# A decoder layer with split weights: weight units of 1024 columns, wider VectorE operations, an order from estimated clocks

## The chip, the cores and the metric

One core of one Trainium2 chip runs the whole layer in one launch. The metric is the device time of that core in microseconds; smaller is better. Four compute engines matter here: TensorE (matmuls and transposes), VectorE, ScalarE and GpSimd; SP's queue and ScalarE's queue issue the DMAs.

## The reference

One layer over 256 tokens and a model width of 2048, all in float32. What is computed, cut to its skeleton:

```python
h = layer_norm(alpha * x + 0.5 * swiglu(x, w_ffn1_gu, w_ffn1_down), ...)      # width 5632
rq, rk, rv, rg, aq, ak, av, gate_r, gate_a = split(h @ w_in)
rq, rk, aq, ak = rotary(...)                                                  # by positions
ret = (silu(rg) * head_group_norm(retention_chunkwise(rq, rk, rv))) @ w_ret_out   # 8 heads
att = sliding_window_attention_sinks(aq, ak, av, sinks) @ w_att_out               # 16 heads
h = layer_norm(alpha * h + (sigmoid(gate_r) * ret + sigmoid(gate_a) * att) @ w_mix_out, ...)
h = layer_norm(alpha * h + 0.5 * swiglu(h, w_ffn2_gu, w_ffn2_down), ...)
h = layer_norm(alpha * h + sigmoid(h @ w_ple_gate) * (p @ w_ple_proj), ...)
```

## The kernel before

**Split numbers.** Every weight and every activation is split into a high part (cast to the matmul's fp32r by ScalarE, line 93) and a low part (VectorE subtracts the high part from the original, line 94). A product of 128 rows, 128 tokens and 512 columns is three matmuls: low by high, high by high, high by low (`Sum.add`, lines 289 to 291). The first of the three needs the low part of the activations and the high part of the weights, the third needs the low part of the weights. All matmuls add in PSUM, one bank of 512 columns for each tile of 128 tokens (t = 0, 1) and block of columns.

**Chunks and sevens.** A weight chunk (`Chunk`) is 1024 values a partition, 4 KB: two rows of 128 by 512 columns. It is loaded by one DMA on SP's queue (line 107), cast and subtracted. A `Single` is one chunk and serves 12 matmuls. A `Seven` is two chunks that are used by a scheme of seven products in place of eight (21 matmuls in place of 24): it needs four sums of weights (lines 165 to 168) that are split too, and forms of the activations (`seven_forms`, lines 360 to 363). Its seven sums lie in the bank pairs of the block and in four banks more, named s; `seven_common` (lines 371 to 374) folds those. In the order of its steps p1, q2, q3, q5, p7, p6, q4, the sums p1, q5, p7 and p6 are the banks named s.

**Stages.** (1) The first feed-forward part, f1: block 0 with plain chunks, while x arrives in four pieces (`first_chunk`, `load_x_chunk`); ten blocks of 512 gate and 512 up columns with three or four sevens in eight (`gu_units`); after each block Silu, a product, and a transposition of the result two side steps later (`turned`: transposes on line 717, ScalarE's copy f1a on line 719). Then two down blocks d0 and d1 with sevens (`down_units`), the last pieces of which are held for the norm. (2) The norm, then the mixers: values (rv), eight groups of queries and keys (rqk) that are rotated (`rotate`: ScalarE copies, VectorE shuffles, GpSimd multiplies), the other values, the retention's gates (rg) with the retention's jobs as side steps, attention's queries and keys (aqk), the gates gt with attention's jobs as side steps, the output projections, and the mix (mo). (3) Norm 1, the second feed-forward part f2, norm 2, the gated embedding (pg), the last norm and the output.

**What sets the order.** The order is written by hand: each engine takes its instructions in the order in which the program issues them, and an engine that waits holds all that stands behind it. `fill` loads and converts chunks ahead of their use. It goes on as long as places of 4 KB are free under a limit that each stage sets (`slots_for_weights`), up to 45 us of TensorE work converted and 90 us loaded. `done` gives places back. `run_side` issues one side job after each chunk; the tables for the rotation (`rotary_tables`, lines 631 to 658, tiles rotr and rota) run there from block 0 of f1 on.

**The norms** (`Norm`). The last three pairs of rows of d1 (six chunks), or the last six chunks of the mix, are held: first all products of token tile 0, then those of tile 1. Behind the first half stand the combination with the residual, the statistics, the moments (`ln_stats`, a chain of nine small operations) and the scaling (`ln_normal`, lines 471 and 472) of tile 0. Its transposes (`ln_turn`, line 479, tile lnps) stand at fixed places among the products of tile 1, and those of tile 1 among the first six chunks of the next stage (`Norm.first`). Each transposed group is split into the activations of the next stage (ht). Between a norm and the mixers, and between norm 1 and f2, stands the projection of p (`put_by`, 24 matmuls).

Places: 46 of 4 KB in SBUF, and PSUM's eight banks as eight single tiles.

Of the kernel before, what the change touches and what calls it, by code (L numbers as in the profile page):

```python
# [8 lines left out]
F32 = mybir.dt.float32  # L9
# [17 lines left out]
KF = FF // P  # L27


HELD_MIX, HELD_END = 6, 8  # L30
FRONT = 6
FRONT_PAIRS = 3
HELD_PAIRS = 3
SLOTS = 46


SEVEN = (0, 1, 2, 3)


# [9 lines left out]

@with_exitstack  # L50
def layer(ctx: ExitStack, tc: tile.TileContext, io):
    nc = tc.nc
    sync, act, dve, pool, pe = nc.sync, nc.scalar, nc.vector, nc.gpsimd, nc.tensor
# [4 lines left out]
    small = ctx.enter_context(tc.tile_pool(name="small", bufs=3))  # L58
    dram = ctx.enter_context(tc.tile_pool(name="dram", bufs=1, space=bass.MemoryType.DRAM))
    psum = ctx.enter_context(tc.tile_pool(name="psum", bufs=8, space=PSUM))  # L60

    def bank(name):
        return psum.tile([P, 512], F32, tag="ps", name=name)

    def banks(name):
        return [bank(name + str(j)) for j in range(2)]
# [4 lines left out]
    def half(name):  # L71
        return slot([P, 2, 256], F32, name)

    plan = []

    def chunk_of(key):


        name, at = key[0], key[1:]
        if name.endswith("_gu"):
            j, gu, c = at
            w = io[name][2 * j : 2 * j + 2, gu, c // 2, :, c % 2 * 2 : c % 2 * 2 + 2, :]
            return w.rearrange("g p k n -> p g (k n)")
        if name[-1] == "2":
            j, c = at
            w = io[name[:-1]][j : j + 2, c // 2, :, c % 2 * 2 : c % 2 * 2 + 2, :]
            return w.rearrange("g p k n -> p g (k n)")
        return io[name][at]  # L90

    def split(dst_hi, dst_lo, src, lo_engine=None):
        act.copy(dst_hi, src)  # L93
        (lo_engine or dve).tensor_tensor(dst_lo, src, dst_hi, ALU.subtract)  # L94

    class Chunk:


        def __init__(self, key, pieces=1, queue=None):
            src = chunk_of(key)  # L100
            self.key, self.paired = key, key[0].endswith("_gu") or key[0][-1] == "2"
            self.name = "_".join(map(str, key))
            self.raw = slot(list(src.shape), F32, "r" + self.name)
            n = src.shape[2] // pieces
            self.parts = [slice(j * n, j * n + n) for j in range(pieces)]
            for at in self.parts:
                (queue or sync).dma_start(self.raw[:, :, at], src[:, :, at])

        def make_hi(self):
            self.hi, self.lo = (slot(list(self.raw.shape), F32R, w + self.name) for w in "hl")  # L110

        def make_part(self, at):
            split(self.hi[:, :, at], self.lo[:, :, at], self.raw[:, :, at])

        def make(self):
            self.make_hi()
            split(self.hi, self.lo, self.raw)

        def of(self, v, kk):

            if self.paired:
                return v.rearrange("p g (k n) -> p g k n", k=2)[:, :, kk, :]
            return v[:, kk, :]

        def columns(self, kk):
            return self.of(self.hi, kk), self.of(self.lo, kk)

    class Single:


        loads, makes, keeps, time = 1, 2, 2, 12

        def __init__(self, key):
            self.key = key

        def load(self, **how):
            self.chunk = Chunk(self.key, **how)

        def make(self):
            self.chunk.make()  # L140

    class Seven:

        loads, makes, keeps, time = 2, 6, 7, 21

        def __init__(self, key, other):
            self.key, self.other = key, other  # L150

        def load(self):
            self.a, self.b = Chunk(self.key), Chunk(self.other)

        def make(self):
            a, b = self.a, self.b
            nm = a.name
            b11, b21, b12, b22 = a.of(a.raw, 0), a.of(a.raw, 1), b.of(b.raw, 0), b.of(b.raw, 1)
            u, v = (slot([P, 2, 512], F32, w + nm) for w in "uv")

            def shaped(x):
                return x.rearrange("p (g n) -> p g n", g=2) if a.paired else x

            t1, t3, t2, t4 = (shaped(x) for x in (u[:, 0], u[:, 1], v[:, 0], v[:, 1]))
            dve.tensor_tensor(t1, b11, b12, ALU.add)
            dve.tensor_tensor(t3, b12, b22, ALU.add)  # L166
            dve.tensor_tensor(t2, b11, t3, ALU.add)
            dve.tensor_tensor(t4, t2, b21, ALU.add)  # L168

            def parted(name, x):  # L170
                hi, lo = (slot([P, 2, 512], F32R, w + name + nm) for w in "hl")
                split(hi, lo, x)
                return [(hi[:, e], lo[:, e]) for e in range(2)]

            a.make()
            self.b11, self.b21 = a.columns(0), a.columns(1)
            both = slot([P, 2, 512], F32R, "b" + nm)
            self.b22 = both[:, 0], both[:, 1]
            split(shaped(both[:, 0]), shaped(both[:, 1]), b22)
# [27 lines left out]
    def take(key):  # L207
        if not ready:
            fill()
# [1206 lines left out]
```

## Time and profile before

| what | value |
|---|---|
| runs, us | 2327.76, 2331.27, 2330.24 |
| median, us | 2330.24 |
| profiled execution: span from the first to the last instruction, us | 2330.8 |
| its granted TensorE clock, mean | 0.992 |
| instructions | 28659 |
| DMA moved | 465.70 MB, mean 200 GB/s |

For the profiled execution the span is the only time that is on record; it lies among the three runs. The page of the profile gives busy times by engine, the stretch of the span cut in 40 slices, the chain of work that ended last and the costliest groups. In a group's row stand line, engine, operation, the tile written and those read (buffer numbers left out), shape, count, then busy time, mean duration of one and the idle time before them. A row of waits has the engine and line that waited, whom it waited for, the total, the number of times and the longest. A row of stages has the stretch, its length, for each engine its busy time and number of instructions, the granted clock, the DMA share and GB/s. A row of the timeline has the start, the time, and the instruction; a bracket names idle time before it.

### The profile page before, as it was taken

How to read it: one execution, taken by the hardware profiler on the slowest of the kernel's cores; microseconds unless marked ns; L12 is line 12 of the kernel's file. 1: busy time of each engine (PE TensorE's matmuls, PEld its weight loads, DVE VectorE, ACT ScalarE, POOL GpSimd, SP SyncE). 2: the span in 40 equal slices, each digit the busy share in tenths (PEclk: the TensorE clock that was granted, in tenths of full speed). 3: DMA queues.
4: the chain of work that ended last, by engine and by line, in shares of the span. 5: the costliest groups of instructions: out<-in, count | busy, mean ns of one | idle time of the engine just before them, and what ended most of it. 6: DMA issues, size and time to landing. Idle time of an engine off the chain costs nothing.

```text
span 2330.8 us, 28659 instructions
## 1 busy us (share of the span) xinstructions
PE 2286.1 (98%) x10490; PEld 1890.7 (81%) x10490; DVE 1884.6 (81%) x2372; ACT 1167.0 (50%) x1412; POOL 97.0 (4%) x53
## 2 busy tenths in 40 slices
PE   9999999999998999999999999999999999999997
PEld 7788888887887888888778888778888888878776
DVE  7999999988978774677655555779999999899866
ACT  5555555655544342434554543355555555555432
POOL 0000000000000530133000000000000000000000
PEclk9999999999999999999999999999999999999999
DMA  9465665664686565546555666576566666465851
GB/s 321 156 215 181 207 205 184 198 217 159 220 296 234 179 226 163 171 144 201 158 158 181 190 207 228 183 245 214 183 190 208 185 206 227 166 210 204 329 190 55
DMA packets 193725, 465.70 MB, mean 200 GB/s; under 512 B 14768, under 2 KB 16048, under 8 KB 193584
## 3 DMA queue, kind: packets, MB, share of 16 engines
q1 hardware_dynamic: 191456, 460.91, 59.7%
q10 hardware_dynamic: 2128, 2.97, 0.4%
q8 instruction: 82, 1.34, 0.2%
q14 instruction: 59, 0.48, 0.1%
HBM read 455.43 MB, written 8.39 MB: 199 GB/s over the span
## 4 chain that ended last, share of the span: by engine, by line
PE 93%; DVE 5%; DMA 1%; issue 1%; ACT 0%; SPq 0%; DVEq 0%; ACTq 0%
PE f2g L291 3%; PE f2g L289 3%; PE f2g L290 3%; PE f1g L289 3%; PE gt L289 3%; PE f1g L290 3%; PE f1g L291 3%; PE rqk L240 3%; PE gt L290 3%; PE gt L291 3%; PE f2u L289 2%; PE f2u L290 2%; PE f2u L291 2%; PE f1u L291 2%; PE f1u L289 2%; PE f1u L290 2%
## 5 line engine op out<-in xcount | busy, mean ns | idle before, releaser
L94 DVE TENSOR_TENSOR lf_gu<-rf_gu,hf_gu 128x1024 fp32r<-128x1024 f32 (+1 forms) x283 | 335.1, 1215 | 11.5 <-ACT hf_gu L93 10.9
L93 ACT CAST hf_gu<-rf_gu 128x1024 fp32r<-128x1024 f32 (+1 forms) x283 | 282.9, 1046 | 17.1 <-DMA rf_gu<-in_f_gu 13.3
L94 DVE TENSOR_TENSOR lw_in_f<-rw_in_f,hw_in_f 128x1024 fp32r<-128x1024 f32 x148 | 208.2, 1439 | 61.7 <-ACT hw_in_f L93 58.5
L94 DVE TENSOR_TENSOR lf_down<-rf_down,hf_down 128x1024 fp32r<-128x1024 f32 x148 | 174.5, 1219 | 14.0 <-ACT hf_down L93 12.0
L93 ACT CAST hf_down<-rf_down 128x1024 fp32r<-128x1024 f32 x148 | 149.4, 1051 | 49.7 <-DMA rf_down<-in_f_down 9.9
L93 ACT CAST huf_gu<-uf_gu 128x1024 fp32r<-128x1024 f32 x70 | 73.8, 1054 | 160.1 <-DVE uf_gu L166 153.5
L93 ACT CAST hw_in_f<-rw_in_f 128x1024 fp32r<-128x1024 f32 x148 | 146.0, 1053 | 0.2
L289 PE MATMUL gt<-hw_in_f,ht 128*128 128x512 f32 x256 | 102.5, 400 | 0.0
L289 PE MATMUL f1g<-hf_gu,xt 128*128 128x512 f32 x247 | 97.0, 393 | 5.5 <-ACT hf_gu L93 5.5
L290 PE MATMUL gt<-hw_in_f,ht 128*128 128x512 f32 x256 | 99.9, 390 | 0.0
L291 PE MATMUL gt<-lw_in_f,ht 128*128 128x512 f32 x256 | 99.9, 390 | 0.0
L290 PE MATMUL f1g<-hf_gu,xt 128*128 128x512 f32 x247 | 96.8, 392 | 0.0
L291 PE MATMUL f1g<-lf_gu,xt 128*128 128x512 f32 x247 | 96.6, 391 | 0.0
L289 PE MATMUL f2g<-hf_gu,ht 128*128 128x512 f32 x247 | 96.4, 390 | 0.0
L291 PE MATMUL f2g<-lf_gu,ht 128*128 128x512 f32 x247 | 96.2, 389 | 0.0
L290 PE MATMUL f2g<-hf_gu,ht 128*128 128x512 f32 x247 | 96.1, 389 | 0.0
L93 ACT CAST hvf_gu<-vf_gu 128x1024 fp32r<-128x1024 f32 x70 | 73.9, 1055 | 29.2 <-DVE vf_gu L168 29.2
L94 DVE TENSOR_TENSOR luf_gu<-uf_gu,huf_gu 128x1024 fp32r<-128x1024 f32 x70 | 85.3, 1219 | 0.0
L94 DVE TENSOR_TENSOR lvf_gu<-vf_gu,hvf_gu 128x1024 fp32r<-128x1024 f32 x70 | 85.3, 1219 | 0.0
L289 PE MATMUL f2u<-hf_gu,ht 128*128 128x512 f32 x212 | 84.0, 396 | 0.0
L289 PE MATMUL f1u<-hf_gu,xt 128*128 128x512 f32 x212 | 83.4, 393 | 0.0
L290 PE MATMUL f2u<-hf_gu,ht 128*128 128x512 f32 x212 | 83.0, 392 | 0.0
(1053 smaller groups left out, 6257.3 us busy)
## 6 DMA issues: line engine op xcount, KB each, us to landing
rf_gu<-in_f_gu SPq DMA_DIRECT2D x351, 512.0 KB, 5.0
rf_down<-in_f_down SPq DMA_DIRECT2D x176, 512.0 KB, 4.6
rw_in_f<-in_w_in_f SPq DMA_DIRECT2D x148, 512.0 KB, 4.2
rw_rv<-in_w_rv SPq DMA_DIRECT2D x32, 512.0 KB, 5.1
rw_ret<-in_w_ret SPq DMA_DIRECT2D x32, 512.0 KB, 4.5
rw_mix<-in_w_mix SPq DMA_DIRECT2D x32, 512.0 KB, 4.5
rw_pg<-in_w_pg SPq DMA_DIRECT2D x32, 512.0 KB, 4.4
rw_att<-in_w_att SPq DMA_DIRECT2D x16, 512.0 KB, 4.3
```

Source lines behind the costliest of these rows:

```text
L93: act.copy(dst_hi, src)
L94: (lo_engine or dve).tensor_tensor(dst_lo, src, dst_hi, ALU.subtract)
L240: pe.matmul(ps[f], hi[:, kk, f * P : (f + 1) * P], rhs(k), start=k == 0, stop=k == n_k - 1,)
L289: pe.matmul(o, al, bh, start=first, stop=False)
L290: pe.matmul(o, ah, bh, start=False, stop=False)
L291: pe.matmul(o, ah, bl, start=False, stop=self.left == 0)
```

## The change

- **Units.** SBUF has 23 places of 8 KB in place of 46 of 4 KB. A unit is 2048 values a partition: two rows of 128 by 1024 columns (both column blocks at once), loaded by two DMAs, or by four shorter-run ones for a seven of the gate and up weights; one cast of 2048, one subtraction of 2048, 24 matmuls. A seven's weights are made in four steps with wider operations. PSUM is four tiles of two banks.
- **Order.** Two estimated clocks, one for TensorE and one for VectorE, are advanced by the sizes of what is issued. Steps of the making of weights are issued while VectorE's clock is behind TensorE's (`pump`), and `after` does so up to the point at which a result of TensorE is expected, ahead of VectorE's work on it. At most three units are loaded ahead.
- **Norms.** What happens behind which held step is a list of events (c combine, m moments, s scale, t transpose, with token tile and group); groups are eight tiles of 128 wide, in norm 1 at first four. Three units are held, four of the next stage stand in front.
- **Moved.** The rotary tables go from f1's first blocks behind norm 0, into the remaining four units of the first value block. The rotation's products go from GpSimd to VectorE, the retention's product with its gate goes to VectorE and ScalarE. The load of p goes from SP's queue at the norm to ScalarE's queue at the start.
- **Start and end.** The first unit comes in four pieces on ScalarE's queue, interleaved with x's first four; other units wait in SP's queue behind x's chunks. At the end five units are held; tile 0 finishes 1024 columns behind them, tile 1 twice 512.

The number of matmuls and transposes stays, and so do the sevens (`SEVEN`, `SEVEN_DOWN`, `SEVEN_BOTH`).

The core of the diff:

```diff
-SLOTS = 46
+SLOTS = 23
+FRONT = 4
+HELD = 3
+HELD_END = 5
+MATMUL = 0.227
+GROUPS = (((0, 8), (8, 8)), ((0, 8), (8, 8)), ((0, 4), (4, 4), (8, 8)))
...
+EVENTS = (
+    {
+        "a6": "c0 m0 s00", "b6": "t00 c1 m1 s10", "c4": "s01", "c6": "t10", "d1": "s11", "d4": "t01", "d7": "t11",
+    },
...
+    {
+        "a6": "c0 m0 s00 s01", "b4": "t00", "b6": "t01 c1 m1 s10 s11", "c4": "s02", "c6": "t10", "c7": "t11",
+        "d1": "s12", "d4": "t02", "d7": "t12",
+    },
+)
...
-    psum = ctx.enter_context(tc.tile_pool(name="psum", bufs=8, space=PSUM))
+    psum = ctx.enter_context(tc.tile_pool(name="psum", bufs=4, space=PSUM))
...
+    def banks(name):
+        return psum.tile([P, 2, 512], F32, tag="ps", name=name)
...
+    class Unit:
+        loads, makes, keeps, steps = 1, 2, 2, 1
...
+        def make(self):
+            self.make_hi()
+            split(self.hi, self.lo, self.raw)
+            spend(2048)
+            yield
...
+    class Seven(Unit):
+        loads, makes, keeps, steps = 1, 5, 4, 4
...
+            act.copy(hb, raw[:, 1:])
+            dve.tensor_tensor(u[:, 0:2], raw[:, 1:3], raw[:, 0:1].broadcast_to([P, 2, 512]), ALU.add)
+            act.copy(hu[:, 0:2], u[:, 0:2])
+            spend(1024)
+            yield
+            dve.tensor_tensor(u[:, 2], raw[:, 2], u[:, 0], ALU.add)
+            dve.tensor_tensor(u[:, 3], u[:, 2], raw[:, 3], ALU.add)
+            act.copy(hu[:, 2:], u[:, 2:])
+            spend(512, 512)
+            yield
...
+            dve.tensor_tensor(lb, raw[:, 1:], hb, ALU.subtract)
+            spend(1536)
+            yield
+            dve.tensor_tensor(lu, u, hu, ALU.subtract)
+            spend(2048)
...
+    clock = {"pe": 0.0, "dve": 0.0}
+    room = {"slots": 0, "used": 0, "far": 3}
+    def spend(*sizes):
+        for n in sizes:
+            clock["dve"] += (n + 150) / 960
...
+    def pump(t):
+        load()
+        while clock["dve"] < t and step():
+            pass
+    def fill():
+        pump(clock["pe"])
+    def after(t=None):
+        t = clock["pe"] if t is None else t
+        pump(t)
+        clock["dve"] = max(clock["dve"], t)
+    def take(*key):
+        load()
+        while not ready:
+            assert step(), (key, room)
+        u = ready.pop(0)
+        clock["pe"] = max(clock["pe"], u.made)
+        return u
...
+            if aux is None:
+                pair = [banks(f"{name}{b}s{j}") for j in range(2)]
+                aux = p1, p6, p7, q5 = [Sum(pair[j // 2][:, j % 2], len(sevens)) for j in range(4)]
...
-            later(2, lambda j=j, v=v: turned(j, v))
+            later(1, lambda j=j, u=u: turned(j, u))
...
-                    if u == 2:
-                        load_constants()
-                        lazy.append(rotary_tables())
+                    if u == 2:
+                        load_constants()
...
+        def held(self, name, b, ps, lhs):
+            us = [take(name, b, p) for p in ps]
+            for j in range(2 * len(ps)):
+                at = j % len(ps)
+                some_products(us[at], ps[at], lhs, self.sums, (0,), (j // len(ps),))
+                fill()
+                run_side()
+                self.at("a", j + 1)
...
-        pool.tensor_tensor(q, q, c, ALU.mult)
-        pool.tensor_tensor(qs, qs, s, ALU.mult)
-        pool.tensor_tensor(dst, q, qs, ALU.add)
+        dve.tensor_tensor(q, q, c, ALU.mult)
+        dve.tensor_tensor(qs, qs, s, ALU.mult)
+        dve.tensor_tensor(dst, q, qs, ALU.add)
...
+        ps, sums = norm.front("w_rv", 0, rhs, plain(PAIRS))
+        lazy.append(rotary_tables())
+        plain_block("w_rv", 0, rhs, start=FRONT, sums=sums)
...
+                        dve.scalar_tensor_tensor(
+                            o[:, e, t], ps[:, e, t * DV : t * DV + DV], mv[:, j, 0:1], g, ALU.subtract, ALU.mult
+                        )
+                        act.mul(o[:, e, t], o[:, e, t], rs[:, j : j + 1])
```

1305 lines of the change are left out of this document (618 added, 687 removed).

## The prediction

> **What bounds the kernel now.** First the page's busy shares, then two matmuls of TensorE's timeline that stand 20 matmuls apart, then TensorE's waits.
>
> ```profile
> PE 2286.1 (98%) x10490; PEld 1890.7 (81%) x10490; DVE 1884.6 (81%) x2372; ACT 1167.0 (50%) x1412; POOL 97.0 (4%) x53
> ```
> ```profile
> 12.85 0.39 PE L289 MATMUL f1g<-hf_gu,xt 128*128 128x512 f32 x1
> ...
> 17.39 0.39 PE L291 MATMUL f1u<-lf_gu,xt 128*128 128x512 f32 x1
> ```
> ```profile
> PE lnps L479 <- DVE f2y L472: 6.6, 5, 3.8
> PE lnps L479 <- DVE f1y L472: 6.1, 4, 2.6
> ...
> PE f11s L289 <- ACT f1a L719: 5.3, 1, 5.3
> PE lnps L479 <- DVE mixy L472: 3.9, 4, 2.7
> ```
>
> A busy 0.39 hides pipelining: (17.39 - 12.85) / 20 = **0.227 us a matmul** of 512 columns. TensorE is nearly full, and its named waits are few: the three norms (transposes waiting for VectorE's scaled rows) and one in the first block with sevens. Now the stages.
>
> ```profile
> 5.00:50.00 45.00, 44.48 (x188) 36.31 (x189) 36.65 (x54) 24.98 (x29) 0.00 (x0) 1.00 0.96 333
> 50.00:75.00 25.00, 19.68 (x85) 15.95 (x84) 23.89 (x37) 13.56 (x18) 0.00 (x0) 0.93 0.40 138
> 100.00:500.00 400.00, 400.00 (x1807) 332.21 (x1806) 375.60 (x435) 227.27 (x258) 0.00 (x0) 1.00 0.62 199
> 555.00:600.00 45.00, 43.40 (x189) 34.97 (x188) 42.15 (x48) 24.87 (x27) 0.00 (x0) 1.00 0.68 232
> 700.00:740.00 40.00, 33.92 (x145) 26.73 (x144) 37.33 (x67) 17.08 (x25) 0.00 (x0) 0.87 0.47 169
> ...
> 1490.00:1525.00 35.00, 31.10 (x144) 24.50 (x143) 31.03 (x59) 17.00 (x28) 0.00 (x0) 0.95 0.52 178
> ...
> 2195.00:2240.00 45.00, 38.24 (x160) 30.05 (x159) 37.20 (x66) 12.22 (x17) 0.00 (x0) 0.89 0.68 244
> ```
>
> The columns: length, busy TensorE, weight loads, VectorE, ScalarE, GpSimd, granted clock, DMA share, GB/s. What a stage loses is its idle TensorE time plus (1 - clock) x length: 5.3 + 1.75 = **7.1** in 50 to 75, 6.1 + 5.2 = **11.3** in norm 0, 3.9 + 1.75 = **5.7** in norm 1, 6.8 + 5.0 = **11.7** in norm 2. That is 36 us, and nearly all that can be won in the middle: from 100 to 500 TensorE idles for nothing although VectorE is 94% busy. The diff keeps every matmul and transpose, so the rest of the span stands.
>
> **The change, part by part.** *Wider operations.* Rows of 512 and of 1024 give the slope.
>
> ```profile
> L94 DVE TENSOR_TENSOR lf_gu<-rf_gu,hf_gu 128x1024 fp32r<-128x1024 f32 x281 | 333.7, 1219 | 9.5 <-ACT hf_gu L93 9.0
> L93 ACT CAST hf_gu<-rf_gu 128x1024 fp32r<-128x1024 f32 x281 | 281.6, 1049 | 15.3 <-DMA rf_gu<-in_f_gu 11.5 <-PE mo L291 1.7 <-PE mo L290 1.4
> ...
> L165 DVE TENSOR_TENSOR uf_gu<-rf_gu,rf_gu 128x512 f32<-128x512 f32 x70 | 47.9, 685 | 0.0
> ...
> L93 ACT CAST bf_gu<-rf_gu 128x512 fp32r<-128x512 f32 x70 | 43.3, 619 | 0.0
> ```
>
> VectorE: 0.151 + 1.043 per 1000 elements, so 2048 take 2.29 and 1536 1.75; ScalarE: 1.91 and 1.48. A plain unit falls from 2 x 1.219 = 2.44 to 2.29, a seven from 7.1 (four of 0.69, four subtractions) to 1.22 + 1.38 + 1.75 + 2.29 = 6.64. Blocks of four sevens and blocks of three alternate: 85.1 us of VectorE a pair of blocks before, with the fold; 79.6 after. The 94% becomes 88%. **I cost this at nothing**: TensorE hid the greater load already. If a margin were lost, it would cost what the down stage loses (555 to 600: 1.6 idle), whose runs of three sevens I leave at 0 (-3 to +3): 6.64 against 21 x 0.227 = 4.77 of TensorE still falls behind there, with about one seven of lead, as now. DMAs carry the same bytes in shorter runs for the sevens; at a DMA share of 0.62 I take 0, and no more than a few us if the share rose to 0.96.
>
> *First block.* The first unit comes in four pieces and needs two for its first product, and each later unit is cast whole.
>
> ```profile
> 4.85 0.62 ACT L93 CAST hf_gu<-rf_gu 128x512 fp32r<-128x512 f32 x1 [1.51 <-DMA rf_gu<-in_f_gu]
> ...
> 6.09 0.62 ACT L93 CAST hf_gu<-rf_gu 128x512 fp32r<-128x512 f32 x1 [0.31 <-DMA rf_gu<-in_f_gu]
> ...
> 12.11 1.05 ACT L93 CAST hf_gu<-rf_gu 128x1024 fp32r<-128x1024 f32 x1 [0.31 <-DMA rf_gu<-in_f_gu]
> ```
> ```profile
> 5.52 0.79 PE L289 MATMUL f1g<-hf_gu,xt 128*128 128x512 f32 x1 [5.52 <-ACT hf_gu L93]
> ```
>
> The second piece is cast at 6.09 now, so the first matmul moves from 5.52 to about 6.8: +1.3. By 12.1 six half-megabytes have landed; in the new order these are x's first two chunks and units 0 and 1. Unit 1's cast then ends at 14.1, its low part at 16.4; TensorE ends unit 0 near 13.3 and waits 2.5, plus one half-clock stretch, which by the rows (25 x 0.07) costs 1.75. Sum **+5.5** (+1 to +8). Against this the rotary tables leave the stage.
>
> ```profile
> 20.00:50.00 30.00, 6.75 (x19) 0.84 (x2) 1.00 0.94 323
> ```
> ```profile
> 50.00:150.00 100.00, 6.76 (x19) 0.83 (x2) 0.98 0.58 190
> ```
> ```profile
> pos_i<-in_positions ACTq DMA_DIRECT2D x1, 128.0 KB, 6.0
> ```
>
> The first row is VectorE and ScalarE on tile rotr alone, the second on rota. Without them, VectorE ends the first seven of block 1 near 46 us plus waits and TensorE gets there at 60: the wait of 7.1 goes, **-7** (-3 to -7).
>
> *Rotary, moved into the first value block behind norm 0.* 14.5 us of VectorE, four waits for ScalarE's sine and the landing of pos_i (6.0, in order, all of VectorE behind it) go into four units, 21.8 us of TensorE, beside 9.2 of splits: some 30 against 22, with one or two units (5 to 11 us) of lead. **+3** (0 to +9). The load of p moves from SP's queue ahead of norm 0 to ScalarE's at the start, 0.26 MB among some 15: 0. The rotations move from GpSimd to VectorE: per group 2 x 2.29 + 5 x 0.69 = 8.0 under 11.2 of TensorE, 0.
>
> *Norms.* The rows are norm 2's, VectorE's timeline.
>
> ```profile
> 2206.02 0.68 DVE L837 TENSOR_TENSOR f2y<-f2y,f2e 128x512 f32<-128x512 f32 x1
> 2206.74 0.69 DVE L500 BATCH_NORM_STATS2 f2st<-f2y 128x6 f32<-128x512 f32 x1
> 2207.47 0.26 DVE L462 BATCH_NORM_AGGREGATE mv<-f2st 128x2 f32<-128x24 f32 x1
> ...
> 2209.42 0.48 DVE L471 SCALAR_TENSOR_TENSOR f2y<-f2y,mv,ln_g 128x256 f32<-128x256 f32 x1
> ...
> 2212.58 0.73 DVE L471 SCALAR_TENSOR_TENSOR f2y<-f2y,mv,ln_g 128x512 f32<-128x512 f32 x1
> ...
> 2225.80 4.63 DVE L94 TENSOR_TENSOR lw_pg<-rw_pg,hw_pg 128x1024 fp32r<-128x1024 f32 x4
> ```
>
> The new chain for tile 0: combine 1.22, two statistics 1.4, moments 1.95 (2207.47 to 2209.42), two scalings of 1024 at 0.74 + 0.53: 7.2 us under the 36 matmuls, 8.2, of tile 1's held half. The four splits of 4.63 that stand in tile 1's chain now are held back by the estimated clock; one of 2.29 at most remains. So the transposes find their rows. Behind them stand a ScalarE cast of 1.05 and a subtraction of 1.22 before the next product: in norms 0 and 1 the per-layer projection's 24 matmuls (5.45) lie over that, in norm 2 nothing does, 2.4 us of wait. Norm 0: 11.3 to 3, **-8** (-4 to -10); norm 1 asks for its first rows at 5.45 and has them at 6.3, 5.7 to 2.5, **-3** (0 to -5); norm 2: 2.4 + 1.75 + 1 for the second tile = 5.2, **-6.5** (-2 to -9). [...]
>
> *PSUM in four pairs.* In each block with sevens the transposed activations take the pair that the fourth product of the first seven needs.
>
> ```profile
> 150.37 0.87 PE f1t L717 x8
> ```
> ```profile
> 152.21 1.06 ACT L93 CAST huf_gu<-uf_gu 128x1024 fp32r<-128x1024 f32 x1 [2.69 <-DVE uf_gu L166]
> 153.66 1.06 ACT L93 CAST hvf_gu<-vf_gu 128x1024 fp32r<-128x1024 f32 x1 [0.40 <-DVE vf_gu L168]
> 154.63 1.06 ACT L719 COPY f1a<-f1t 128x512 f32<-128x512 f32 x2
> ```
>
> Here ScalarE copies 3.4 us after the last transpose, behind two casts that wait for VectorE; 24 matmuls cover it. After, 9 matmuls do: 2.04. The estimated clock issues a cast at most one step ahead of TensorE and the copy takes 1.05, so I take 0.1 a block: **+2** (0 to +24, below). The gate blocks free pairs as well: a Silu of 1024, about 1.1 by the cast rows, behind 0 to 1.9 of cast, with 1.36 or no cover, twice: **+2.5** (0 to +7).
>
> *Tail.* After the last product:
>
> ```profile
> 2317.32 0.69 DVE L1220 TENSOR_TENSOR sg<-sg,ppr 128x512 f32<-128x512 f32 x1 [0.86 <-ACT sg L1219]
> ```
>
> Tile 0's last norm now has 1024 columns to finish, 1.1 + 2.44 + 1.4 + 1.95 + 8 x 0.77 = 13.1 us under 13.6 of matmuls, and tile 1's first half (2.1) behind it: **+1** (0 to +3).
>
> Sum: 5.5 - 7 + 3 - 8 - 3 - 6.5 + 2 + 2.5 + 1 = -10.5. The profiled span is 2330.8, the median of three 2330.24, 0.6 lower: 2330.8 - 10.5 - 0.6 = **2320**.
>
> **Rivals.** (1) *The pairs of PSUM bind.* If half of the twenty seven-blocks show the present 3.4, each waits 3.4 + 1.05 - 2.04 = 2.4, +24, and 1.75 more where the clock falls: against -12.5 without that term, 2342 to 2359. It decides where ScalarE starts the copy more than 1.0 behind the last transpose. For it: every second block shows 3.4. Against: a VectorE that is 6% freer. [...] (2) *The backlog moves*: rotary at 9, start at 8, gates at 7 and norms at half their gain: 9 + 8 + 7 - 7 - 9 = +8, 2338; half of the way there is 2329, no change (2326 to 2335). Here too stands that the estimated clocks do not order the chain as meant, since splits issued ahead run whenever their places are free. (3) *All waits go*: -7 - 10 - 5 - 9 with 5 for the start and the rest at 0 is -26, **2304**.
>
> **How the numbers follow.** My forecast 0.48 (2312 to 2325), rival 3 0.10, rival 2 0.17, rival 1 0.25. So faster 0.58, same 0.17, slower 0.25, 0.2% (4.7 us) being about what a measurement tells from no change. The range leaves out a tenth at each side: the best part of rival 3 and rival 1 beyond 2344, so 2302 to 2344.
>
> **What would show it.** In the new profile: no wait in 50 to 75 but one of 2 to 3 us near 14; the transposes of the norms (tile lnps) waiting under 1 us each for VectorE, and at norm 2 one wait of 2.4 of the first product for the split of ht; granted clock over 0.95 in norm 0; VectorE near 88% from 100 to 500. Wrong would be: a wait in every block of the product named s for ScalarE's copy of the activations, or waits for the weights' low parts in the value and rotation blocks.

## The result, and the profile after

| | before | after |
|---|---|---|
| median of four runs, us | 2330.57 | 2308.24 |
| lowest and highest, us | 2327.76, 2331.27 | 2305.40, 2308.92 |
| profiled span, us | 2330.8 | 2306.3 |
| granted clock, mean | 0.992 | 0.996 |

The ratio is 0.9904, with a 95% interval from 0.989 to 0.9918: 22.3 us faster by the medians, 24.5 by the profiled spans. The profile of before overstates it: wherever an execution's own time is on record, its span is 1.7 to 2.1 us shorter than that time (2306.3 for 2308.07 here), so the profiled execution of before, with a span of 2330.8, took some 2332.6, longer than all four of its runs. What its stages lose is therefore some 2 us on the high side. The forecast was 10.5. Its sign and its range held; its size did not.

First the busy line of the page of the changed kernel, then its stages, for the stretches that the prediction showed of before (those of the norms shifted and of other lengths, since the norms come earlier and take less time now) and for two more. The columns are those of the prediction: length, TensorE, weight loads, VectorE, ScalarE, GpSimd, clock, DMA share, GB/s.

```profile
PE 2275.3 (99%) x10490; PEld 1885.7 (82%) x10490; DVE 1802.4 (78%) x1571; ACT 1128.9 (49%) x922; POOL 0.7 (0%) x6
```
```profile
5.00:50.00 45.00, 42.03 (x168) 33.74 (x168) 31.76 (x24) 26.00 (x20) 0.00 (x0) 0.96 0.95 339
50.00:75.00 25.00, 25.00 (x116) 20.80 (x115) 24.19 (x20) 14.26 (x13) 0.00 (x0) 1.00 0.57 171
100.00:500.00 400.00, 399.61 (x1804) 331.40 (x1803) 360.36 (x262) 221.71 (x172) 0.00 (x0) 1.00 0.61 200
555.00:600.00 45.00, 42.52 (x187) 34.32 (x186) 41.55 (x30) 24.69 (x19) 0.00 (x0) 1.00 0.54 192
690.00:730.00 40.00, 40.00 (x186) 33.30 (x185) 34.45 (x42) 14.58 (x11) 0.00 (x0) 1.00 0.72 270
730.00:760.00 30.00, 30.00 (x142) 24.98 (x141) 27.80 (x37) 14.70 (x11) 0.00 (x0) 1.00 0.72 259
1490.00:1530.00 40.00, 38.42 (x180) 31.41 (x180) 35.39 (x33) 23.30 (x18) 0.00 (x0) 1.00 0.61 211
2055.00:2075.00 20.00, 17.63 (x71) 13.86 (x70) 17.81 (x13) 11.84 (x9) 0.00 (x0) 0.91 0.62 224
2183.00:2225.00 42.00, 40.56 (x194) 32.91 (x192) 36.18 (x48) 10.70 (x9) 0.00 (x0) 1.00 0.74 284
```

Read as in the prediction, idle TensorE time plus (1 - clock) x length is what a stage loses. The first block with sevens (50 to 75) went from 7.1 to 0, norm 0 (690 to 730) from 11.3 to 0, norm 1 from 5.7 to 1.6, norm 2 from 11.7 to 1.4: **32.8 us** came from these four. The start now loses 2.97 + 1.8 = 4.8 where it lost 0.5, and the first down block of the second feed-forward part (2055 to 2075) loses 2.37 + 1.8 = 4.2, where before TensorE was busy for all 20 at full clock. Between the first and the last matmul as a whole, TensorE idles 10.7 us where it idled 25.0, and half clock costs 3.4 where it cost 13.7. TensorE's waits name the rest:

```profile
PE f1g L324 <- ACT hf_gu L84: 6.4, 2, 6.0
PE f_down0s L326 <- DVE luf_down L188: 2.5, 2, 1.2
PE f_down0s L326 <- DVE lbf_down L185: 2.4, 2, 1.2
PE f1g L326 <- DVE lf_gu L85: 1.6, 1, 1.6
PE f_gu L324 <- DVE ht L85: 1.6, 2, 0.9
```

The first row is mainly the first matmul (6.0); the fourth is the second unit's low part at the start, which the prediction expected near 14; rows two and three are the sevens of the down blocks. The transposes (tile lnps), which led this list before, wait for VectorE nowhere.

**One statement of the sections before the prediction is wrong, and the prediction rests on it.** The lists of groups and events are counted from norm 0, so the groups of four belong to norm 2, behind the second feed-forward part, and not to norm 1.

### The profile page after: what moved, and what is told of

It reads as the page before. It is cut to its first block, busy times and chain, and to the rows that moved or that the text cites. A ratio compares the mean times of both kernels' runs of the same rounds, so it can differ in the third digit from the quotient of the medians.

```text
span 2306.3 us, 26593 instructions
## 1 busy us (share of the span) xinstructions
PE 2275.3 (99%) x10490; PEld 1885.7 (82%) x10490; DVE 1802.4 (78%) x1571; ACT 1128.9 (49%) x922; POOL 0.7 (0%) x6
## 4 chain that ended last, share of the span: by engine, by line
PE 94%; DVE 3%; DMA 1%; issue 1%; ACT 0%; SPq 0%; DVEq 0%; ACTq 0%
PE f1g L326 5%; PE f1g L324 5%; PE f1g L325 5%; PE f2g L324 4%; PE f2g L325 4%; PE f2g L326 4%; PE rqk L288 3%; PE aqk L288 2%; PE f2d L324 1%; PE f2d L325 1%; PE f2d L326 1%; PE ga L324 1%; PE f1e L326 1%; PE f1e L325 1%; PE f1e L324 1%; PE gr L324 1%
## 5 line engine op out<-in xcount | busy, mean ns | idle before, releaser
L85 DVE TENSOR_TENSOR lf_gu<-rf_gu,hf_gu 128x2048 fp32r<-128x2048 f32 (+1 forms) x109 | 239.9, 2228 | 49.6 <-ACT hf_gu L84 48.9
L84 ACT CAST hf_gu<-rf_gu 128x2048 fp32r<-128x2048 f32 (+1 forms) x109 | 200.2, 1861 | 37.4 <-DMA rf_gu<-in_f_gu 15.6
L324 PE MATMUL f1g<-hf_gu,xt 128*128 128x512 f32 x424 | 166.7, 393 | 6.8 <-ACT hf_gu L84 6.4
L325 PE MATMUL f1g<-hf_gu,xt 128*128 128x512 f32 x424 | 166.4, 392 | 0.0
L188 DVE TENSOR_TENSOR luf_gu<-uf_gu,huf_gu 128x2048 fp32r<-128x2048 f32 x70 | 160.0, 2286 | 1.6
L85 DVE TENSOR_TENSOR lf_down<-rf_down,hf_down 128x2048 fp32r<-128x2048 f32 x60 | 136.4, 2288 | 25.1 <-ACT hf_down L84 18.2
L324 PE MATMUL f2g<-hf_gu,ht 128*128 128x512 f32 x360 | 140.1, 389 | 0.4 <-DVE eve L407 0.4
L325 PE MATMUL f2g<-hf_gu,ht 128*128 128x512 f32 x360 | 140.1, 389 | 0.0
L84 ACT CAST hf_down<-rf_down 128x2048 fp32r<-128x2048 f32 x60 | 113.8, 1910 | 44.0 <-DMA rf_down<-in_f_down 22.8
L185 DVE TENSOR_TENSOR lbf_gu<-rf_gu,hbf_gu 128x1536 fp32r<-128x1536 f32 x70 | 122.7, 1752 | 13.2 <-ACT hbf_gu L174 13.1
L174 ACT CAST hbf_gu<-rf_gu 128x1536 fp32r<-128x1536 f32 x70 | 103.5, 1479 | 22.3 <-DMA rf_gu<-in_f_gu 17.5
L324 PEld LDWEIGHTS f1g<-hf_gu,xt 128*128 128x128 f32 x424 | 80.5, 190 | 24.3 <-ACT hf_gu L84 6.8
L325 PEld LDWEIGHTS f1g<-hf_gu,xt 128*128 128x128 f32 x424 | 80.3, 189 | 16.7
```

Of the source, the lines that this page charges most:

```text
L85: dve.tensor_tensor(dst_lo, src, dst_hi, ALU.subtract)
L174: act.copy(hb, raw[:, 1:])
L185: dve.tensor_tensor(lb, raw[:, 1:], hb, ALU.subtract)
L188: dve.tensor_tensor(lu, u, hu, ALU.subtract)
L324: pe.matmul(o, al, bh, start=first, stop=False)
L325: pe.matmul(o, ah, bh, start=False, stop=False)
```

## The experiments

Each run is set against the kernel before by its ratio, and against its base by medians: 2308.24 for the changed kernel, for the kernel before its own median beside that run (2330.1 to 2331.0). All differences are in us. The four runs of the changed kernel lie 3.5 apart, and the intervals of the ratios leave some 3 us to each side, so a difference of about 1 shows nothing by itself.

| run | base | median | ratio to before (95%) | against its base |
|---|---|---|---|---|
| rotary tables early | changed | 2317.25 | 0.9939 (0.9927 to 0.9951) | +9.0 |
| no clock | changed | 2348.87 | 1.0089 (1.0074 to 1.0103) | +40.6 |
| norm 2 in eights | changed | 2308.76 | 0.9904 (0.989 to 0.9917) | +0.5 |
| narrow | changed | 2311.14 | 0.9914 (0.9901 to 0.9928) | +2.9 |
| narrow, same clock | changed | 2308.05 | 0.9902 (0.9887 to 0.9918) | -0.2 |
| start in halves | changed | 2307.17 | 0.99 (0.9885 to 0.9915) | -1.1 |
| down order | changed | 2303.39 | 0.9886 (0.9873 to 0.99) | -4.9 |
| halves and order | changed | 2302.78 | 0.9881 (0.9868 to 0.9895) | -5.5 |
| front of three | changed | 2315.66 | 0.9942 (0.9929 to 0.9954) | +7.4 |
| tile 0 first | changed | 2322.17 | 0.9962 (0.9948 to 0.9976) | +13.9 |
| rotary tables late | before | 2322.54 | 0.9969 (0.9958 to 0.9981) | -7.6 |
| splits held back | before | 2329.38 | 0.9997 (0.9989 to 1.0006) | -0.7 |
| wide front | before | 2330.42 | 1.0002 (0.9993 to 1.001) | -0.1 |
| joint | before | 2330.53 | 0.9999 (0.999 to 1.0008) | +0.1 |
| late transposes | before | 2322.39 | 0.9961 (0.9948 to 0.9974) | -8.7 |

**The rotary tables.** Put back into the changed kernel, and taken out of the kernel before (there with twelve side steps behind each of the last two chunks of the first value block):

```diff
# changed kernel
+                        lazy.append(rotary_tables())   # at unit 2 of f1's first block
-        lazy.append(rotary_tables())                   # behind norm 0
# kernel before
-                        lazy.append(rotary_tables())   # in f1's first block
+        lazy.append(rotary_tables())                   # behind norm 0's front
```

> The changed kernel with the rotary tables put back into the first feed-forward part, from its first block on. Theory (the 7.0 us of the first block with sevens went because the tables, 14.5 us of VectorE with four waits, left that stage): a wait of TensorE for f1s or for a low part returns between 50 and 75, +3 to +7 us over the changed kernel, and the stretch 730 to 760 shows VectorE near 18 of 30 busy instead of 27.8. Rival (the new order of the weight steps took the wait away, whatever stands beside it): 50 to 75 stays without a wait, 0 (-1 to +1).

> The kernel before with the rotary tables moved behind norm 0, into the first value block. Theory (the tables alone made the 7.1 us of 50 to 75): -7 (-5 to -7.5) if their new place costs nothing, and up to +9 of waits there if the place is as dear as the forecast's upper bound. Rival (the order of the splits made that wait): 50 to 75 stays as it is, 0 or slower.

The kernel before with late tables, from 50 to 75 and over norm 0 with the value block; then the kernel before itself over the latter:

```profile
50.00:75.00 25.00, 25.00 (x116) 20.78 (x115) 24.36 (x30) 15.00 (x18) 0.00 (x0) 1.00 0.68 197
...
690.00:760.00 70.00, 63.18 (x300) 50.79 (x299) 61.10 (x116) 27.42 (x41) 0.00 (x0) 0.98 0.61 224
```
```profile
690.00:760.00 70.00, 63.92 (x284) 51.82 (x283) 51.45 (x80) 27.26 (x36) 0.00 (x0) 0.93 0.68 257
```

The 7.1 of 50 to 75 are gone with nothing but the tables moved, and the stretch that takes them loses no more than before (8.2 against 11.0; it idles 0.7 more, at a higher clock), with VectorE at 61 of 70. So the move is worth 7.6 alone. In the changed kernel the early tables cost 9.0, but for the most part at another place than the theory said: 50 to 75 idles only 1.3, and the start loses 5.5 + 3.6 = 9.1 in place of 4.8. The first down block loses 2.2 more (560 to 640), and behind norm 0 comes a wait of 1.4. VectorE's 18 of 30 from 730 to 760 did not come either (27.0): the norm stands later in that run, and its chain fills the stretch. Its start and its first block with sevens:

```profile
5.00:50.00 45.00, 39.52 (x150) 31.12 (x151) 34.75 (x56) 21.48 (x21) 0.00 (x0) 0.92 0.97 343
50.00:75.00 25.00, 23.66 (x109) 19.34 (x107) 22.56 (x20) 13.10 (x13) 0.00 (x0) 1.00 0.41 121
```

**The width of VectorE's operations**, with the estimated clock charged for what is issued, then as in the changed kernel:

```diff
-            split(self.hi, self.lo, self.raw)
-            spend(2048)
+            act.copy(self.hi, self.raw)
+            for c in range(2):
+                at = slice(2 * c, 2 * c + 2)
+                dve.tensor_tensor(self.lo[:, at], self.raw[:, at], self.hi[:, at], ALU.subtract)
+            spend(1024, 1024)          # the second of the two runs: spend(2048)
...
```

The sums and subtractions of the sevens are cut in the same way.

> The changed kernel with VectorE's operations on weights cut back to 1024 and 512 elements, the casts left whole; the same elements are worked on. Theory (in the steady blocks VectorE lies beside TensorE and width is worth nothing): VectorE from 90% to about 95% busy in 100 to 500 and still no wait there, 0 to +3 us from the runs of sevens in the down stages. Rival (the width of the operations is the gain): +10 to +20 us.

> The changed kernel with VectorE's operations on weights cut to 1024 and 512 as in the narrow run, but the estimated clock charged as for the wide ones, so that the order of the steps stays that of the changed kernel. Theory (the 8.3 us that norm 2 lost in the narrow run came from the order alone, a split put ahead of the combination and waiting for a place, and the narrow operations cost nothing of themselves): no wait of 8 us at norm 2, the start and the down stages as in the narrow run, -3 to -7 us against the changed kernel. Rival (narrow operations make VectorE late at the norm): +1 to +4, with the wait at norm 2.

The width of VectorE's operations is worth nothing that these runs can tell: with the order kept, 2308.05 against 2308.24. VectorE is busy for 366.7 of 400 us from 100 to 500 in the first of them (about 95% was expected) and TensorE for all 400. The casts stayed wide in both runs, so the width of the casts was not tested. What the first narrow run lost, it lost at one place, norm 2. VectorE's timeline there, then TensorE's:

```profile
2188.94 2.36 DVE L130 TENSOR_TENSOR lw_pg<-rw_pg,hw_pg 128x1024 fp32r<-128x1024 f32 x2 [9.35 <-issue]
2191.22 1.21 DVE L803 TENSOR_TENSOR f2y<-f2y,f2e 128x1024 f32<-128x1024 f32 x1
```
```profile
2188.68 0.39 PE L333 MATMUL f2e<-lf_down,f2ac 128*128 128x512 f32 x1
2197.33 1.12 PE L498 MATMUL lnps<-ident,f2y 128*128 128x128 f32 x4 [8.26 <-DVE f2y L466]
```

VectorE stands idle 9.35 us before a split that it then does just as TensorE ends its run of held products, and tile 0's combination is queued behind that split. The trace names no releaser; a place that TensorE's products still hold fits, but this is inferred. With the same operations charged as wide ones, the split is issued elsewhere and the wait is gone. The -3 to -7 of the theory did not come, though: the start loses 1.5 in place of 4.8 (2.3 in the narrow run), but 100 to 500 now idles 2.5.

**The estimated clock.**

```diff
-        while clock["dve"] < t and step():
+        while step():
```

> The changed kernel with weight steps issued as early as there is room, not bounded by VectorE's estimated clock. Theory (the three norms got short because the clock keeps the splits of later weights out of the chains of the norms): the transposes lnps wait for VectorE again and the clock falls there, +3 to +5 us at norm 2, +2 to +4 at each of the others, +7 to +12 in all; and the activations' copies of the blocks with sevens stand behind more casts. Rival (room is the true bound, three units loaded ahead): the order hardly changes, 0 (-1 to +2).

It costs 40.6, about four times what the theory said, and the norms are the smaller part: they lose some 12 us more than in the changed kernel. Waits, then two stages:

```profile
PE w_rv L324 <- DVE ht L85: 5.2, 1, 5.2
PE f1g L324 <- DVE eve L405: 4.3, 2, 2.5
PE f1t L681 <- DVE eve L730: 3.6, 2, 2.3
PE f2t L681 <- DVE eve L730: 3.3, 2, 2.1
```
```profile
100.00:500.00 400.00, 389.68 (x1745) 320.35 (x1745) 350.14 (x253) 211.99 (x165) 0.00 (x0) 1.00 0.61 197
...
1540.00:2040.00 500.00, 489.76 (x2197) 403.01 (x2196) 436.06 (x319) 268.15 (x206) 0.00 (x0) 1.00 0.60 196
```

The blocks with sevens idle 10.3 and 10.2 us in these two stretches, where the changed kernel idles 0.4 in each: VectorE's folds (eve L405) and its products ahead of the transposes (L730) stand behind splits; TensorE needs the PSUM that the first set free, and transposes what the second make. At norm 0 w_rv waits 5.2 for ht. So the clock serves the steady blocks more than the norms.

**Norm 2's groups.**

```diff
-GROUPS = (((0, 8), (8, 8)), ((0, 8), (8, 8)), ((0, 4), (4, 4), (8, 8)))
+GROUPS = (((0, 8), (8, 8)), ((0, 8), (8, 8)), ((0, 8), (8, 8)))
```

> The changed kernel with norm 2 in groups of eight transposes and with the event list of norm 0, in place of its groups of four. Theory (the split of the first eight tiles of ht, a ScalarE cast and a subtraction, is uncovered in norm 2, as forecast, and the groups of four took that wait away): one wait of 2 to 2.8 us of the first product of the per-layer gate for ht, with or without a stretch of half clock, +2 to +4.5 us. Rival (other work covers it): 0 (-1 to +1).

```profile
2201.48 0.80 PE L323 MATMUL w_pg<-hw_pg,ht 128*128 128x512 f32 x1 [2.36 <-DVE ht L84]
```

The wait of 2.4 us that the prediction worked out is there, to a few hundredths, once norm 2 has the groups that the prediction gave it. The median moved by 0.5 only, less than the two runs can tell: the first down block of the second part lost 1.4 less in this execution.

**The norms, part by part, in the kernel before.** No splits among the first chunks behind a norm; norm 0's front over two value blocks; both, with a front of eight chunks; and then also the transposes in the order of the changed kernel:

```diff
# held back
                 tokens_chunk(u.chunk, k0, lhs, [sums[t][n] for t in range(2)], (0,))
-                fill()
# wide front
+        steps = [(("w_rv", n, c), 2 * c, n) for c in range(KD // 2) for n in range(2)]
+        norm.first(steps[:FRONT], rhs, sums, (2, 3, 4, 6))
...
# joint: both, and
-FRONT = 6
+FRONT = 8
# late transposes: the joint run, and in norms 0 and 1 (tile 0's, then tile 1's and tile 0's last two groups)
-        norm.run(steps, lhs, (8, 9, 11, 12))
+        norm.run(steps, lhs, (12, 12))
-        norm.first(steps, rhs, sums, (2, 3, 4, 6))
+        norm.first(steps, rhs, sums, (6, 8, 14, 16), ((11, 2), (12, 3)))
```

> The kernel before, changed in one place: among the first six chunks behind a norm no further chunks are split, so that the splits leave the chain of tile 1. Theory (the norms of before lose their time to splits that stand in the chain of tile 1): the transposes lnps wait less in all three norms, -6 to -13 us against the kernel before, less what the stages behind the norms then wait for splits that were not made. Rival (the chain itself and the groups of transposes are the loss, and the splits only fill the gaps): 0 (-2 to +3).

> The kernel before with the first two value blocks made side by side behind norm 0, so that its first six chunks ask for 6 rows of the normed activations in place of 12 in the same time. Theory (the pace at which the front asks for transposed rows sets the loss of a norm; norm 1, whose front is 1024 columns wide already, loses 6.1 us where norms 0 and 2 lose 11.2 and 12.6): norm 0 falls from 11.2 to about 6, -4 to -6 us. Rival (the splits in VectorE's chain set it, and they stay): 0 (-1 to +1).

> The kernel before with three things at once: no further splits among the first chunks behind a norm, a front of eight chunks in place of six, and the first two value blocks side by side behind norm 0. Each of the first and the last alone changed nothing. Theory (a norm is covered only where the front is long and the splits stay out, as in the changed kernel, where a front of three units gave 7.4 us back): norms 0 and 1 fall from 11.2 and 6.1 to 3 to 6 and 2 to 4, -7 to -13 us in all. Rival (the estimated clock's order within the norm is needed, and the splits find their way back into the chain of tile 1 through the places that the held chunks give back): -3 to +2.

> The joint run's kernel with one thing more in norms 0 and 1: the transposes of tile 0 stand behind all held products of tile 1, and those of its third and fourth group behind the chain of tile 1, among the products of the long front. Theory (the place of the transposes, with the front that permits it, is what the norms gained from): against the joint run norm 0 from 12.2 to 3 to 7 and norm 1 from 7.5 to 2 to 5, -6 to -13 us against the kernel before. Rival (without the estimated clock the splits of the next stage fill the gap that is left): -2 to +2.

Three misses in a row, then a hit. Waits of the run with splits held back:

```profile
PE lnps L479 <- DVE f1y L472: 3.6, 5, 1.6
PE lnps L479 <- DVE f2y L472: 3.5, 5, 1.6
PE lnps L479 <- DVE mixy L472: 1.7, 4, 0.7
PE rv L289 <- ACT hw_rv L93: 1.6, 1, 1.6
PE f2g L289 <- ACT hf_gu L93: 1.6, 1, 1.6
PE pg L289 <- ACT hw_pg L93: 1.4, 1, 1.4
```

The transposes wait 8.8 us in all where they waited 16.6, but the next stage now waits for weights that were not made, in pieces and partly at half clock, and the time stays. The wide front alone leaves norm 0 as it was, since its transposes still stand at their old places. Norm 0 and norm 1 of the joint run, and then of the one with late transposes:

```profile
690.00:760.00 70.00, 64.01 (x273) 51.03 (x272) 55.49 (x83) 30.45 (x39) 0.00 (x0) 0.93 0.70 262
1480.00:1540.00 60.00, 55.83 (x250) 44.29 (x249) 53.58 (x82) 28.27 (x39) 0.00 (x0) 0.97 0.65 228
```
```profile
690.00:760.00 70.00, 66.52 (x308) 54.58 (x307) 55.13 (x82) 30.37 (x39) 0.00 (x0) 1.00 0.70 271
1480.00:1540.00 60.00, 56.30 (x263) 46.14 (x262) 47.07 (x76) 25.74 (x37) 0.00 (x0) 1.00 0.64 224
```

Norm 0 loses 3.5 in place of 10.9, norm 1 3.7 in place of 6.0, and the run is 8.7 faster than the kernel before. The splits were held back in both, and the clock's order is in neither: it is the **place of the transposes**. With each of them the program of before also issues VectorE's scaling of the next group, so this work moved behind tile 1's chain too; which of the two counts for more was not separated, nor was the late place tried without the longer and wider front.

**The same, taken out of the changed kernel.** Second group of tile 0 ahead of tile 1's chain, in norms 0 and 1; and a front of three units:

```diff
# tile 0 first
-        "a6": "c0 m0 s00", "b6": "t00 c1 m1 s10", "c4": "s01", "c6": "t10", "d1": "s11", "d4": "t01", "d7": "t11",
+        "a6": "c0 m0 s00", "b6": "t00 s01 t01 c1 m1 s10", "c6": "t10", "d1": "s11", "d7": "t11",
...
# front of three; the events of part d move up with it
-FRONT = 4
+FRONT = 3
...
```

> The changed kernel with the second group of tile 0 scaled, transposed and split ahead of tile 1's chain in norms 0 and 1, as all groups of tile 0 stand in the kernel before; in the changed kernel they stand behind it. Theory (it is this order, which a front that asks for half of the rows permits, that keeps TensorE busy at the norms): tile 1's chain is 5 to 6 us later, waits for ht or lnps return at norms 0 and 1, +2 to +6 us at each. Rival (the chain of tile 1 has slack, and the held-back splits are what counts): 0 (-1 to +1).

> The changed kernel with three units in place of four in front behind each norm (16.3 us of TensorE for both tiles, as before, in place of 21.8), the transposes of the second groups moved up with it. Theory (the longer front covers the chain of tile 1 and the second groups): waits for ht or lnps return, +2 to +5 us at each of the three norms, +6 to +13 in all. Rival (the front is long enough at three, and the width of 1024 columns does it): 0 (-1 to +2).

TensorE at norm 0 with tile 0 first, then VectorE:

```profile
710.71 1.03 PE L491 MATMUL lnps<-ident,f1y 128*128 128x128 f32 x8
716.66 1.94 PE L491 MATMUL lnps<-ident,f1y 128*128 128x128 f32 x8 [4.92 <-issue]
```
```profile
713.96 1.28 DVE L458 SCALAR_TENSOR_TENSOR f1y<-f1y,mv,ln_g 128x1024 f32<-128x1024 f32 x1
715.27 1.28 DVE L459 SCALAR_TENSOR_TENSOR f1y<-f1y,rstd,ln_b 128x1024 f32<-128x1024 f32 x1
...
720.83 1.21 DVE L796 TENSOR_TENSOR f1y<-f1y,f1e 128x1024 f32<-128x1024 f32 x1
```

The second group's transposes stand where VectorE has no rows for them until 716.5: 4.9 us of wait here, 6.0 at norm 1, and half clock behind both (this execution is the slowest of the five, 4 us above their median). Tile 1's combination comes at 720.83; in the changed kernel it starts at 713.87. The cost is not quite where the expectation put it (it is the early transposes themselves that wait, not tile 1's), and larger, 13.9. A front of three costs 7.4: the waits for ht behind the three norms are 2.4, 3.4 and 2.0, where the changed kernel has 0, 1.6 and 0.6.

**The two places that got worse.**

```diff
# start: units 1 to 3 in halves
+            n = 2 if self.key in HALVED else 4
+            for c in range(0, 4, n):
+                split(self.hi[:, c : c + n], self.lo[:, c : c + n], self.raw[:, c : c + n])
# down blocks: order of the last ten units of d0
+        first = first[:12] + [(kinds[p], p) for p in (12, 13, 14, 17, 15, 16, 20, 18, 19, 21)]
```

> The changed kernel with units 1 to 3 of the first block cast and split in two halves of 1024. Theory (the whole unit's cast of 1.9 and subtraction of 2.3 us are what TensorE waits for at 13.2 and 14.5): those 2.3 us fall under 0.7 and the half clock behind them goes, -2 to -4 us. Rival (the arrival of the units is what bounds the start): 0 (-1 to +1).

> The changed kernel with the first down block's last sevens spread among plain units, so that at most two stand in a row. Theory (a seven is 6.6 us of VectorE under 4.8 of TensorE, and a row of three outruns the lead): the waits of 3.1 us near 578 and of 4.3 near 2066 go, -4 to -7 us. Rival (the lead is short there because of what is done before, the last block's activations): the waits move to the first seven, 0 (-2 to +2).

> The changed kernel with both of its cheap repairs: units 1 to 3 of the first block made in halves, and the first down block's last sevens spread. The first alone took 3.7 us off the start but 1.1 off the median, the second 4.9 off the median. If the two add: 2302 to 2304 by the medians, 2299 to 2300 by the stages. Rival (the halves only move the wait into the blocks behind, as the 0.9 that appeared at 100 suggests): 2303 to 2305.

The down order took 4.9 off: with at most two sevens in a row the waits of f_down0s are gone, and 2.2 us of waits in the second down blocks are what has come in their place. Halves take the start from 4.8 to 1.75 idle at full clock, all of it ahead of the first matmul, but the median moves by 1.1. Both repairs together reach 2302.78, 0.6 under the order alone: inside the theory's 2302 to 2304, and 0.2 below the rival's 2303 to 2305, so the median does not decide between them. The stages speak for the rival: in the run with both, 100 to 500 idles 2.3 in place of 0.4, so about half of the start's gain is given back in the blocks behind. Part of the start's loss is also chance: the run with the down order alone did not touch the start, and it lost 2.4 there, at full clock. The kernel with both has the lowest median here, 5.5 under the changed one.

## Why the prediction was right or wrong

| step | forecast | measured by the stages |
|---|---|---|
| start | +5.5 | +4.3, of it the first matmul +0.4 (+1.3 forecast) |
| first block with sevens | -7 | -7.1 |
| rotary tables behind norm 0 | +3 | 0 |
| norm 0 | -8 | -11.3 |
| norm 1 | -3 | -4.1 |
| norm 2 | -6.5 | -10.3 |
| PSUM pairs, blocks with sevens | +2 | +0.8 |
| gate blocks | +2.5 | no loss there before or after |
| tail | +1 | +0.2 (from TensorE's last start to the end 14.55, then 14.74) |
| down runs of sevens | 0 | +3.5 |

**The stages were named rightly; the step that failed is the size of the norms.** The forecast left 3, 2.5 and 5.2 us at the three norms, a gain of 17.5; the stages show 0, 1.6 and 1.4 left, a gain of 25.7. Two terms that stood on no wait (rotary tables +3, gate blocks +2.5) added to the shortfall, and one failed against it, the down blocks, which were put at 0 and lost 3.5. So 10.5 was forecast and 22.3 measured. And the reason given for the norms is not the whole one, as the next paragraph says.

*"Norm 0: 11.3 to 3"* and *norm 2, "2.4 + 1.75 + 1 for the second tile"* failed. The residues had three sources. The 2.4 and its 1.75 at norm 2 came from giving norm 2 the groups of norms 0 and 1; the run in eights shows the 2.36 where the prediction had it, so the arithmetic held and the reading of the list did not. The 1 to 3 for the second tile stood on no row, and TensorE waits for VectorE's rows nowhere now. And the reason given, splits kept out of tile 1's chain, is not enough: the run that held splits back halved the waits of the transposes but gained nothing, nor did the joint run; the late transposes gained 8.7 without the estimated clock, and the reverse cost 13.9. The event list asks for a group's transposes only when VectorE has its rows, and a front of four units 1024 columns wide asks for half of the rows for 21.8 us; the prediction read the list for tile 0's first group alone. That the clock's order adds to this at norm 0 is shown too (5.2 of wait without it).

*"Rotary, some 30 against 22: +3"* failed. The tables' place costs nothing in the changed kernel (VectorE at 27.8 of 30 from 730 to 760, no wait) and nothing in the kernel before. VectorE pays in the rotation groups behind what it owes there. In the run with early tables, where these stages stand 9 us later, VectorE is busy for 10.8 of 15 us from 754 to 769 and for 4.6 of 20 from 769 to 789; the changed kernel has 13.8 and 14.7 for the same stages, 13 us more, with TensorE busy throughout in both.

*"The Silu of the gate blocks: +2.5"* had no row of a wait behind it, and no wait came: from 900 to 1100 TensorE is busy 200.00 of 200 in both kernels.

*"I take 0.1 a block"* held. In all twenty blocks with sevens ScalarE's copy now starts 0.0 to 0.1 us behind the last transpose, where before every second block showed 3.4; the 0.8 that these blocks lose are waits for VectorE's fold.

*"Runs of three sevens I leave at 0 (-3 to +3)"* failed on the other side, by 3.5. The two first down blocks, before and then in the changed kernel:

```profile
560.00:640.00 80.00, 78.40 (x344) 63.95 (x343) 79.10 (x93) 45.92 (x50) 0.00 (x0) 1.00 0.62 218
2040.00:2120.00 80.00, 78.66 (x345) 64.19 (x344) 74.99 (x87) 43.06 (x46) 0.00 (x0) 1.00 0.56 194
```
```profile
560.00:640.00 80.00, 77.52 (x341) 63.31 (x340) 75.91 (x57) 43.46 (x33) 0.00 (x0) 1.00 0.64 235
2040.00:2120.00 80.00, 77.63 (x336) 63.53 (x335) 75.94 (x56) 43.24 (x34) 0.00 (x0) 0.98 0.59 212
```

They lose 6.4 where they lost 2.9. Of that, 1.6 is one stretch of half clock; of the idle time, 4.9 where before had 2.9, the two narrow runs keep 3.7 and 3.9, so about half of the surplus comes of the wide operations, by one profile each. That three in a row outrun the lead is shown by the down order.

*Wider operations at nothing* was right for the whole (VectorE at 360.36 of 400 from 100 to 500, 90% where 88% was forecast). The last step, from the span to the time, went the wrong way: 0.6 was taken off, while the executions on record took some 1.8 more than their spans, so the same sum should have ended near 2322.

**Rival 1** did not come. Without the clock the time, 2348.87, falls inside its 2342 to 2359, but that is luck: the copy starts late in four of the twenty blocks only (by 1.8 to 3.1), and TensorE's waits for ScalarE's copies are 5.4 us in all, against 16.8 for VectorE's folds and products. **Rival 2** names the mechanism that showed once, in the narrow run: a split put ahead of the chain, 8.3 us. **Rival 3**, all waits gone at 2304, is 4 us from the result and was the best account: its -7, -10, -5, -9 and +5 are each within 1.3 us of the stages, and what it lacks is mainly the down blocks. It had a chance of 0.10.

What stays open: how much of the norms' 25.7 us belongs to the event order, the front and the clock each, since they do not add (13.9 and 7.4 for the first two taken out singly, some 12 at the norms for the clock). In before some 12 of the 25.7 were half clock, and of two waits of 2.36 us in other runs only one had half clock behind it (last section), so another execution of before need not lose as much there.

## What to carry to other kernels

Place a transposition by the time at which its rows are finished: what the next stage needs of the second tile goes ahead of those rows of the first tile that it does not need yet, and a wider or longer front is worth having because it permits that (8.7 us gained here by the late place with such a front, 0.1 lost by the front without it, 13.9 lost by the early place in the changed kernel). Where buffers are few, an order that keeps long optional work behind the short operations that free a buffer is worth more (40 us here) than the width of VectorE's operations (0 here). A term for which no row of the profile shows a wait belongs near zero (+3 and +2.5 were forecast here, and neither loss came), with its far end kept for the range.

## What the runs showed of the hardware

In the clock's records, every stretch of half clock between the first and the last matmul lasts 3.413 us or twice that, and in each of the 17 traces all of them begin a whole number of 3.413 us behind the first record. How long TensorE waited does not decide alone whether one comes. Two waits of one length, from the run with norm 2 in eights (above, at 2201.48) and from the front of three:

```profile
730.79 0.50 PE L324 MATMUL w_rv<-hw_rv,ht 128*128 128x512 f32 x1 [2.36 <-DVE ht L85]
```

The windows of that grid around the first, then around the second:

```profile
2197.69:2201.10 3.41, 1.43 (x11) 1.06 (x9) 3.01 (x2) 1.01 (x1) 0.00 (x0) 1.00 0.95 369
2201.10:2204.51 3.41, 3.03 (x7) 2.45 (x8) 3.27 (x7) 0.00 (x0) 0.00 (x0) 0.50 1.02 413
```
```profile
726.38:729.80 3.42, 2.05 (x14) 1.56 (x12) 0.29 (x1) 1.33 (x2) 0.00 (x0) 1.00 1.02 355
729.80:733.21 3.41, 2.42 (x11) 2.00 (x12) 3.38 (x4) 3.29 (x2) 0.00 (x0) 1.00 0.89 374
733.21:736.62 3.41, 3.41 (x21) 2.92 (x20) 3.41 (x3) 0.54 (x1) 0.00 (x0) 1.00 0.81 269
```

The first wait falls nearly all into one window, in which TensorE idles 2.0 us, and the next window runs at half clock. The second is spread over two windows, with 1.4 and 1.0 us idle, and the clock stays. The same count for all windows of the 17 traces that ran at full clock: behind each of the 39 in which TensorE idled 1.86 us or more came one at half clock, behind none of the 191 with 0.25 to 1.6 us, and behind 8 of the 19 between. So in these traces a window idle for 1.86 of its 3.41 us, somewhat over half, was enough each time. The wait of 2.36 us cost 1.7 us more, half of 3.41, in the one run and nothing in the other, by where the grid fell, and a forecast for this kernel should carry that as a chance.

The records start later than the matmuls. In the changed kernel the first matmul starts at 5.96 and the first record at 9.90; up to there matmuls stand 0.43 us apart in place of 0.227, though the granted clock reads 1.00. In the 17 traces this stretch lasts from 2.9 to 6.0 us.
